# Layer norms in place with GpSimd left only the power, their scale and bias over rows put off to VectorE, and the per-layer input projected from split parts

## The chip, the cores and the metric

The kernel runs on one core of a Trainium2 chip. The metric is the device time of one execution in microseconds (us). The core has TensorE (PE: matmuls, and a separate row for its weight loads, PEld), VectorE (DVE), ScalarE (ACT), GpSimd (POOL), and SyncE (SP), which here only issues transfers.

## The reference

A two-layer decoder on 256 tokens of 1024 channels, in f32. Each layer has a mixer (mLSTM in layer 0, latent attention in layer 1), an expert stage (PEER), and a gated per-layer input. After the mixer and after the expert stage stands a layer norm:

```python
def layer_norm(x, g, b):
    mu = jnp.mean(xf, -1, keepdims=True)
    var = jnp.mean(jnp.square(xf - mu), -1, keepdims=True)
    y = (xf - mu) * lax.rsqrt(var + NORM_EPS)
    return y * g + b
for i in range(DEPTH):
    mix = mlstm_mixer(x, ...) if i < N_A_LAYERS else mla_mixer(x, ...)
    x = layer_norm(DN_ALPHA * x + mix, ln_g[i, 0], ln_b[i, 0])
    x = layer_norm(DN_ALPHA * x + peer_ffn(x, ...), ln_g[i, 1], ln_b[i, 1])
    x = x + jax.nn.sigmoid(x @ ple_w_gate[i]) * (p[i] @ ple_w_proj[i])
```

There are four norms, called N0 (layer 0, after the mixer), N1 (layer 0, after the experts), N2 and N3 (layer 1) below.

## The kernel before

**Numbers.** Every large product is made from two parts of each operand: `split` (L241) casts a weight tile to a rounded part `hi` on ScalarE (L248) and takes the rest, `lo`, by a subtraction (L251), and `mm3` (L258 to L261) adds three matmuls, hi by hi, hi by lo and lo by hi. The subtraction runs on the engine that `lo_engine` names: VectorE, but GpSimd inside a norm.

**Order.** The program is a queue of jobs, `Pipe`. A job is one weight tile's matmuls; its split is issued up to three jobs ahead (`AHEAD`), and a job pushed with `fence=True` (the norms) may not be looked past. After each job its `budget` is spent on fillers: generators that issue one small piece of work at a time. `drain` issues what is left of one. Each engine then works through its instructions in the order in which they were issued.

**Stages.** Per layer: the mixer; the first norm; the query products of the experts (`qps`, over the 8 MB of `w_q`); the top-k and a stage of 64 steps over `u`; a stage of 64 steps over `v` (the value stage, `v_jobs`, four jobs a step, tile `vw`), whose result stays in the four banks `acc`; the second norm, with the projection of the per-layer input `p @ w_pp` inside; and the gate (`gate_jobs`), sixteen jobs over `w_pg` in two halves of eight, each half ended by a sigmoid and two products in `finish` (L1242 to L1244).

**A norm** (`norm_rows`, L419). The two blocks of 128 tokens, tb 0 and tb 1, go through the same steps. `total` (L435) adds ALPHA times the residual to the mixer's or experts' result and writes tile `z`; `stats` takes mean and variance; the power -0.5 is taken on GpSimd (L444); L448 makes -mean times the power. `scale` writes z times the power plus that, for tb 0 on ScalarE (L454) and for tb 1 on VectorE (L452). `turn` transposes eight 128x128 pieces on TensorE (L464), and `first`, `first_rest`, `second` and `second_parts` read them, with the norm's scale and bias now per partition, into the split, transposed `xt` (names x0a, x0b, x1a, x1b with h or l) that the next products read. At the end GpSimd multiplies and adds the scale and bias over the rows of `z` (L538, L539, tile `gb`): these rows are the residual of the next norm, or what the gate is added to. The two or three splits that were issued ahead of the norm have their casts early and their subtractions inside it, on GpSimd.

In a second norm `project` (L1207) makes the four 128x512 products of the per-layer input in plain f32 from `pw` and `pt` (L1210), one ahead of `turn(0)`, one behind it, and two behind `turn(1)`; `keep` copies them out (L1225).

Of the kernel before, what the change touches and what calls it, by code (L numbers as in the profile page):

```python
# [25 lines left out]
D = 1024  # L26
# [137 lines left out]
def tile_trunk(ctx: ExitStack, tc: tile.TileContext, a, out):  # L164
# [74 lines left out]

    lo_engine = Box()  # L240
    lo_engine.v = nc.vector  # L241

    put_off = Box()

    def split(src, n=512, low=None):
        hi = hi4()
        lo = lo4()
        nc.scalar.copy(hi[:, :n], src)  # L248

        def rest():  # L250
            (low or lo_engine.v).tensor_sub(lo[:, :n], src, hi[:, :n].bitcast(F32))  # L251
# [166 lines left out]

    def norm_rows(acc, xres, idx, gb, xt_name, during=()):  # L419

        z = s8("z")
        mvs, sts, banks = {}, {}, {}
# [79 lines left out]
        lows, put_off.v = put_off.v, None  # L502
        lo_engine.v = nc.gpsimd
        total(0, 0)
# [5 lines left out]
        stats(0, 1)  # L510
        lows.pop(0)()
        if not early:
# [8 lines left out]
        stats(1, 1)  # L521
        for fn in lows:
            fn()
        lo_engine.v = nc.vector
        first(0)
# [5 lines left out]
        first_rest(1)  # L531
        second(0)
        second(1)
        second_parts(0)
        second_parts(1)
        during[3]()
        for tb in range(2):
            nc.gpsimd.tensor_mul(rows(tb), rows(tb), gb[:, 0:D])  # L538
            nc.gpsimd.tensor_add(rows(tb), rows(tb), gb[:, D:2 * D])  # L539
        return z, xt  # L540


# [310 lines left out]
    def pre_gb():  # L853
        xres.v = s8("xres")
        load(xres.v, a["x"])
        gbx.v = load_gb(0)

# [3 lines left out]
    def first_norm(idx, name):  # L861
        def run():
            xcur.v, xt.v = norm_rows(acc, xres.v, idx, gbx.v, name)
        return run
# [4 lines left out]

    def peer(l):  # L870
        idx = small([P, 256, 2, 2], "idx", F16)
# [326 lines left out]
    def second_norm(l):  # L1198
        pw, pt = raw("pw"), raw("pt")
        load(pw, a["w_pp"][l])  # L1200
        load(pt[:, 0:512], a["pT"][l])
        if l == 0:
# [4 lines left out]
        def project(tb, hf):  # L1207
            ps = acc_bank()
            for k in range(2):
                nc.tensor.matmul(ps, pt[:, k * 256 + tb * 128:k * 256 + tb * 128 + 128],  # L1210
                                 pw[:, k * D + hf * 512:k * D + hf * 512 + 512], start=(k == 0), stop=(k == 1))
            return ps

        def run():
# [11 lines left out]
            xcur.v, xt.v = norm_rows(acc, xcur.v, 2 * l + 1, gbx.v, "x%db" % l,  # L1226
                                     [step((0, 0)), step((0, 1)), step((1, 0), (1, 1)), keep])
        return run, pp

    def gate_jobs(l, pp, x3):  # L1230

        o = Box()

        def finish(hf, banks):
            if o.v is None:
                o.v = s8("xple")
            if l == 0 and hf == 0:
# [32 lines left out]
        for hf in range(2):  # L1270
            place = pair_of_banks()
            if hf == 0:
                pipe.later(3, lambda: warm(AF.Sigmoid))
            move_jobs(lambda k, n, hf=hf: wgx.v[:, hf * 4096 + k * 512:hf * 4096 + (k + n) * 512],
                      xt, place, list(range(8)), post=lambda hf=hf, place=place: finish(hf, place()),
                      tail=4 if hf else 99)
    def mla(x3):
# [357 lines left out]
```

## Time and profile before

| | |
|---|---|
| median of 3 runs | 1964.25 us (1963.82 to 1964.58) |
| profiled execution | 1963.32 us, its span 1961.2 us |
| TensorE busy | 1903.8 us (97%) |
| VectorE busy | 1486.2 us (76%) |
| ScalarE busy | 1045.2 us (53%) |
| GpSimd busy | 154.1 us (8%) |
| data moved | 336.69 MB, mean 172 GB/s |

All times below are positions and lengths in the span of the profiled execution. The span is cut into stages; in each of them the busy time of an engine divided by the stage's length tells how much room it has. Within a stage the timeline lists the instructions by their start. The bracket at the end of a row is the time for which the engine stood still ahead of it and what let it go on.

### The profile page before, as it was taken

Reading aid. Unit: us, or ns where it says so; the run is one execution under the profiler, and the core shown is the slowest. Engines: PE = TensorE matmul, PEld = TensorE weight load, DVE = VectorE, ACT = ScalarE, POOL = GpSimd, SP = SyncE. Lnnn points to the kernel's source line nnn. Section 1 sums busy time; section 2 is a strip of 40 time slices with the busy share of each in tenths; the row PEclk is TensorE's granted clock in tenths of the full one; section 3 lists DMA queues with packets and bytes.
Section 4 is the critical chain, followed back from the end, with each engine's and each line's share of the span. In section 5 each row is a group of like instructions: output and inputs, shape, how many; then the busy total and the mean of one; then the engine's idle time right before and its main releaser. Section 6 shows DMA issues by size and latency. Waiting matters only on the chain.

```text
span 1961.2 us, 32911 instructions
## 1 busy us (share of the span) xinstructions
PE 1903.8 (97%) x12648; PEld 1713.3 (87%) x12648; DVE 1486.2 (76%) x3100; ACT 1045.2 (53%) x1972; POOL 154.1 (8%) x126
## 2 busy tenths in 40 slices
PE   9989999999999999999899899999999999999997
PEld 7779999999997888888697799899999888888885
DVE  6677999788887666666766789987888866666666
ACT  5555555555445555555564455455554455555554
POOL 0030142000000000000200301510000000000003
PEclk9989999999999999999999899999999999999999
DMA  9241545444434576757143125454444265755550
GB/s 371 102 178 46 185 158 176 169 163 161 163 139 173 193 258 235 259 202 260 62 172 129 43 102 179 151 187 158 162 162 173 101 222 193 279 215 193 193 177 22
DMA packets 50861, 336.69 MB, mean 172 GB/s; under 512 B 5776, under 2 KB 6032, under 8 KB 12688
## 3 DMA queue, kind: packets, MB, share of 16 engines
q1 hardware_dynamic: 50704, 334.59, 47.2%
q8 instruction: 99, 1.62, 0.4%
q14 instruction: 58, 0.48, 0.1%
HBM read 333.52 MB, written 1.05 MB: 171 GB/s over the span
## 4 chain that ended last, share of the span: by engine, by line
issue 67%; PE 18%; DVE 13%; POOL 1%; ACT 0%; DMA 0%; POOLq 0%; SPq 0%; ACTq 0%
DVE lo L251 5%; PE acc L259 2%; PE acc L260 2%; PE acc L261 2%; DVE scr L956 2%; PE qps L297 2%; PE qps L294 2%; PE qps L291 2%; DVE scr L965 1%; DVE z L452 1%; DVE scr L905 1%; PE acc L1010 1%; DVE scr L897 1%; POOL lo L251 1%; DVE scr L902 0%
## 5 line engine op out<-in xcount | busy, mean ns | idle before, releaser
L251 DVE TENSOR_TENSOR lo<-vw,hi 128x512 fp32r<-128x512 f32 x512 | 354.2, 692 | 258.8 <-ACT hi L248 250.6
L248 ACT CAST hi<-vw 128x512 fp32r<-128x512 f32 x512 | 319.3, 624 | 305.4 <-DVE lo L251 267.9
L248 ACT CAST hi<-u 128x512 fp32r<-128x512 f32 x512 | 315.9, 620 | 285.3 <-PE ups L297 255.6
L251 DVE TENSOR_TENSOR lo<-u,hi 128x512 fp32r<-128x512 f32 x512 | 368.8, 729 | 88.9 <-ACT hi L248 86.3
L260 PE MATMUL acc<-lo,wb 128*128 128x512 f32 x1024 | 398.6, 389 | 0.0
L259 PE MATMUL acc<-hi,wb 128*128 128x512 f32 x1024 | 398.4, 389 | 0.0
L261 PE MATMUL acc<-hi,wb 128*128 128x512 f32 x1024 | 398.4, 389 | 0.0
L260 PEld LDWEIGHTS acc<-lo,wb 128*128 128x128 f32 x1024 | 192.2, 188 | 40.4 <-DVE lo L251 0.5
L261 PEld LDWEIGHTS acc<-hi,wb 128*128 128x128 f32 x1024 | 192.2, 188 | 40.0
L259 PEld LDWEIGHTS acc<-hi,wb 128*128 128x128 f32 x1024 | 192.2, 188 | 39.6
L251 DVE TENSOR_TENSOR lo<-h,hi 128x512 fp32r<-128x512 f32 (+2 forms) x178 | 116.2, 665 | 73.6 <-ACT hi L248 71.9
L248 ACT CAST hi<-h 128x512 fp32r<-128x512 f32 (+2 forms) x194 | 115.0, 604 | 105.5 <-PE acc L261 47.7
L294 PE MATMUL ups<-x0ah,lo 128*128 128x256 f32 x1024 | 166.1, 285 | 5.1 <-DVE lo L251 5.1
L294 PE MATMUL ups<-x1ah,lo 128*128 128x256 f32 x1024 | 165.8, 284 | 5.2 <-DVE lo L251 5.2
L291 PE MATMUL ups<-x1ah,hi 128*128 128x256 f32 x1024 | 167.6, 286 | 0.0
L291 PE MATMUL ups<-x0ah,hi 128*128 128x256 f32 x1024 | 167.6, 286 | 0.0
L297 PE MATMUL ups<-x0al,hi 128*128 128x256 f32 x1024 | 164.4, 283 | 0.0
L297 PE MATMUL ups<-x1al,hi 128*128 128x256 f32 x1024 | 164.4, 283 | 0.0
L294 PEld LDWEIGHTS ups<-x0ah,lo 128*128 128x128 f32 x1024 | 141.2, 192 | 7.2 <-DVE lo L251 7.2
L294 PEld LDWEIGHTS ups<-x1ah,lo 128*128 128x128 f32 x1024 | 140.9, 191 | 7.2 <-DVE lo L251 7.2
L291 PEld LDWEIGHTS ups<-x0ah,hi 128*128 128x128 f32 x1024 | 141.3, 192 | 0.0
L291 PEld LDWEIGHTS ups<-x1ah,hi 128*128 128x128 f32 x1024 | 141.2, 192 | 0.0
(357 smaller groups left out, 2662.6 us busy)
## 6 DMA issues: line engine op xcount, KB each, us to landing
u<-u SPq DMA_DIRECT2D x128, 1024.0 KB, 4.8
vw<-v SPq DMA_DIRECT2D x128, 1024.0 KB, 4.8
h<-w_q SPq DMA_DIRECT2D x16, 1024.0 KB, 10.4
h<-w_pg SPq DMA_DIRECT2D x16, 512.0 KB, 5.6
h<-w_v SPq DMA_DIRECT2D x4, 1024.0 KB, 14.3
h<-w_og SPq DMA_DIRECT2D x4, 1024.0 KB, 18.5
h<-w_ao SPq DMA_DIRECT2D x4, 1024.0 KB, 20.6
gb<-lnp SPq DMA_DIRECT2D x4, 1024.0 KB, 5.8
```

What stands on the lines that cost most here:

```text
L248: nc.scalar.copy(hi[:, :n], src)
L251: (low or lo_engine.v).tensor_sub(lo[:, :n], src, hi[:, :n].bitcast(F32))
L259: nc.tensor.matmul(o, lh, rh, start=first, stop=False)
L260: nc.tensor.matmul(o, lh, rl, start=False, stop=False)
L261: nc.tensor.matmul(o, ll, rh, start=False, stop=last)
L291: nc.tensor.matmul(o, hi[:, c:c + 128], x.v.h(k), start=(k == 0), stop=False)
L294: nc.tensor.matmul(o, lo[:, c:c + 128], x.v.h(k), start=False, stop=False)
L297: nc.tensor.matmul(o, hi[:, c:c + 128], x.v.l(k), start=False, stop=(k == nk - 1))
L452: nc.vector.tensor_scalar(v[:, c], v[:, c], mv[:, 2:3], mv[:, 3:4], op0=ALU.mult, op1=ALU.add)
L897: nc.vector.max_index(iu[:, 0:8], v[:, 0:8], s)
L905: nc.vector.max_index(iu[:, 8:16], v[:, 8:16], s)
L956: nc.vector.tensor_tensor(eq, iota[:, None, 0:NCAND].to_broadcast([P, 16, NCAND]), d["pf"][:, h * 16:h * 16 + 16, None].to_broadcast([P, 1 ...
```

## The change

- Norms work in place: `norm_rows` gets the residual tile as `z` and writes its sums back into it, so there is no new tile. L448 goes: tb 0 takes -mean on VectorE (a 128x1 instruction that needs no power) and multiplies it by the power on ScalarE; tb 1 subtracts the mean and multiplies by the power in one instruction.
- GpSimd keeps the power. The subtractions of the splits stay on VectorE: one ahead of `scale(1)`, the others behind `second(0)`.
- The scale and bias over rows become a filler, `affine`, of four VectorE instructions of 128x1024. For N0 and N2 it runs in the value stage of the same layer (`gb` loaded at step 2, used from step 6, and ended by step 32); for N1 and N3 in the gate, whose jobs now have a budget of 900.
- `p @ w_pp` is made with `mm3` from split parts. `w_pp` and `p` are loaded at step 54 of the value stage; `w_pp` is split by a filler from step 58 (four casts, four subtractions), `p` at step 62. The twelve matmuls of tb 0 stand ahead of `turn(0)`, those of tb 1 between `turn(0)` and `turn(1)`, and the copies ahead of `first(1)`.

```diff
-    def norm_rows(acc, xres, idx, gb, xt_name, during=()):
-        z = s8("z")
+    def norm_rows(acc, z, idx, xt_name, during=()):
...
-            nc.vector.scalar_tensor_tensor(rows(tb)[:, c], xres[:, tb * D + hf * 512:tb * D + hf * 512 + 512],
-                                           ALPHA, acc[tb][hf], op0=ALU.mult, op1=ALU.add)
+            nc.vector.scalar_tensor_tensor(rows(tb)[:, c], rows(tb)[:, c], ALPHA, acc[tb][hf],
+                                           op0=ALU.mult, op1=ALU.add)
...
                 nc.gpsimd.tensor_tensor(mv[:, 2:3], mv[:, 1:2], nhalf[:, 0:1], op=ALU.pow)
+                if tb == 0:
+                    nc.vector.tensor_scalar(mv[:, 3:4], mv[:, 0:1], -1.0, None, op0=ALU.mult)
         def scale(tb):
-            nc.vector.scalar_tensor_tensor(mv[:, 3:4], mv[:, 0:1], -1.0, mv[:, 2:3], op0=ALU.mult, op1=ALU.mult)
+            if tb == 0:
+                nc.scalar.activation(mv[:, 3:4], mv[:, 3:4], AF.Copy, scale=mv[:, 2:3])
             for c in (slice(0, 512), slice(512, 1024)):
                 if tb:
-                    nc.vector.tensor_scalar(v[:, c], v[:, c], mv[:, 2:3], mv[:, 3:4], op0=ALU.mult, op1=ALU.add)
+                    nc.vector.tensor_scalar(v[:, c], v[:, c], mv[:, 0:1], mv[:, 2:3],
+                                            op0=ALU.subtract, op1=ALU.mult)
...
-        lo_engine.v = nc.gpsimd
...
-        lows.pop(0)()
...
-        for fn in lows:
-            fn()
-        lo_engine.v = nc.vector
+        lows.pop(0)()
         first(0)
         scale(1)
...
         second(0)
+        for fn in lows:
+            fn()
         second(1)
...
+    def affine(z, gb):
         for tb in range(2):
-            nc.gpsimd.tensor_mul(rows(tb), rows(tb), gb[:, 0:D])
-            nc.gpsimd.tensor_add(rows(tb), rows(tb), gb[:, D:2 * D])
+            v = z[:, tb * D:(tb + 1) * D]
+            nc.vector.tensor_mul(v, v, gb[:, 0:D])
+            yield 1130
+            nc.vector.tensor_add(v, v, gb[:, D:2 * D])
+            yield 1130
...
+        def affine_gen():
+            yield from affine(xcur.v, gbx.v)
+        def load_first():
+            gbx.v = load_gb(2 * l)
+        def use_first():
+            pipe.fillers.append(affs)
         def load_next():
+            pipe.drain(affs)
             gbx.v = load_gb(2 * l + 1)
...
+        def part_gen():
+            ple["wh"], ple["wl"] = s8("pwh", F32R), [xt4("pwl").rearrange("p a b -> p (a b)") for _ in range(2)]
+            for c in range(0, 2048, 512):
+                h, src = ple["wh"][:, c:c + 512], ple["w"][:, c:c + 512]
+                nc.scalar.copy(h, src)
+                nc.vector.tensor_sub(ple["wl"][c // D][:, c % D:c % D + 512], src, h.bitcast(F32))
+                yield 700
...
+            nc.scalar.copy(ple["th"], ple["p"])
+            nc.vector.tensor_sub(ple["tl"], ple["p"], ple["th"].bitcast(F32))
...
+            if pr in (2, 6, 32):
+                pipe.push({2: load_first, 6: use_first, 32: load_next}[pr])
+            if pr in (54, 58):
+                pipe.push(load_ple if pr == 54 else part_ple)
...
+            if pr == 62:
+                pipe.push(part_p)
...
-                nc.tensor.matmul(ps, pt[:, k * 256 + tb * 128:k * 256 + tb * 128 + 128],
-                                 pw[:, k * D + hf * 512:k * D + hf * 512 + 512], start=(k == 0), stop=(k == 1))
+                mm3(ps, ple["th"][:, t], ple["tl"][:, t], ple["wh"][:, c], ple["wl"][k][:, hf * 512:hf * 512 + 512],
+                    k == 0, k == 1)
...
-                                     [step((0, 0)), step((0, 1)), step((1, 0), (1, 1)), keep])
+                             [step((0, 0), (0, 1)), step((1, 0), (1, 1)), keep])
...
+        pipe.push(lambda: pipe.fillers.append(affs))
...
-                      tail=4 if hf else 99)
+                      tail=4 if hf else 99, budget=900.0)
```

VectorE's order in N3, before, from the statistics of tb 1 on (`lnst` and `lnmv` hold the statistics, `xtps` the transposed pieces, `h` is a gate weight tile):

```order
L442 BN_AGGR lnmv<-lnst 128x2
L443 TENSOR_SCALAR lnmv<-lnmv 128x1
L448 SCALAR_TENSOR_TENSOR lnmv<-lnmv 128x1
L452 TENSOR_SCALAR z<-z,lnmv 128x512 x2
L484 TENSOR_TENSOR x1bl_21030<-hi,x1bh_21028 128x4x128
L473 TENSOR_SCALAR hi<-xtps,cols 128x128 x2
L484 TENSOR_TENSOR x1bl_21030<-hi,x1bh_21028 128x4x128
L473 TENSOR_SCALAR lo<-xtps,cols 128x256 x2
L495 TENSOR_TENSOR x1bl_21031<-lo,x1bh_21029 128x512 x2
L251 TENSOR_TENSOR lo<-h,hi 128x512 x10
```

The same place now, where `xple` is the tile of the rows:

```order
L439 BN_AGGR lnmv<-lnst 128x2
L440 TENSOR_SCALAR lnmv<-lnmv 128x1
L248 TENSOR_TENSOR lo<-h,hi 128x512
L452 TENSOR_SCALAR xple<-xple,lnmv 128x512 x2
L485 TENSOR_TENSOR x1bl_21067<-hi,x1bh_21065 128x4x128
L474 TENSOR_SCALAR hi<-xtps,cols 128x128 x2
L485 TENSOR_TENSOR x1bl_21067<-hi,x1bh_21065 128x4x128
L248 TENSOR_TENSOR lo<-h,hi 128x512
L474 TENSOR_SCALAR lo<-xtps,cols 128x256 x2
L496 TENSOR_TENSOR x1bl_21068<-lo,x1bh_21066 128x512 x2
L248 TENSOR_TENSOR lo<-h,hi 128x512 x2
```

L448 is gone, and two of the splits' subtractions stand inside the norm. Behind the last of these rows VectorE's order in the gate was ten subtractions in a row; now it goes on with:

```order
L542 TENSOR_TENSOR xple<-xple,gb 128x1024
L248 TENSOR_TENSOR lo<-h,hi 128x512
L544 TENSOR_TENSOR xple<-xple,gb 128x1024
L248 TENSOR_TENSOR lo<-h,hi 128x512
L542 TENSOR_TENSOR xple<-xple,gb 128x1024
L248 TENSOR_TENSOR lo<-h,hi 128x512
L544 TENSOR_TENSOR xple<-xple,gb 128x1024
L248 TENSOR_TENSOR lo<-h,hi 128x512 x5
```

The four row instructions stand between the subtractions for the first half's jobs 4 to 7.

TensorE's order in N3, before, from the value stage's end to the gate's first product:

```order
L1210 MATMUL acc<-pw,pt 128x512 x2
L464 MATMUL xtps<-ident,z 128x128 x8
L1210 MATMUL acc<-pw,pt 128x512 x2
L464 MATMUL xtps<-ident,z 128x128 x8
L1210 MATMUL acc<-pw,pt 128x512 x4
L259 MATMUL acc<-hi,x1bh_21028 128x512
```

The same place now: the last two of tb 1's four triples (hi by hi, hi by lo, lo by hi of one half of the contraction), the second `turn`, and the gate's first product:

```order
L256 MATMUL acc<-pwh,pt 128x512
L257 MATMUL acc<-pwl,pt 128x512
L258 MATMUL acc<-pwh,pt 128x512
L256 MATMUL acc<-pwh,pt 128x512
L257 MATMUL acc<-pwl,pt 128x512
L258 MATMUL acc<-pwh,pt 128x512
L465 MATMUL xtps<-ident,xple 128x128 x8
L256 MATMUL acc<-hi,x1bh_21065 128x512
```

Nothing of the projection stands behind the second `turn` any more.

## Rows read from the trace of the kernel before

**Rows 1.** The page, busy time of each engine.
```profile
PE 1903.8 (97%) x12648; PEld 1713.3 (87%) x12648; DVE 1486.2 (76%) x3100; ACT 1045.2 (53%) x1972; POOL 154.1 (8%) x126
```
**Rows 2.** Stages: length, busy PE, PEld, DVE, ACT, POOL; clock, DMA, GB/s.
```profile
112.00:136.00 24.00, 15.67 (x69) 12.32 (x67) 20.42 (x25) 11.04 (x21) 15.96 (x10) 0.72 0.29 117
1600.00:1900.00 300.00, 300.00 (x1325) 248.43 (x1324) 186.21 (x277) 166.10 (x276) 0.00 (x0) 1.00 0.59 212
```
**Rows 3.** Timeline of N3: start, length, engine, line, operation, tiles, [idle, releaser].
```profile
1916.27 0.39 PE L261 MATMUL acc<-hi,wb 128*128 128x512 f32 x1
1920.51 0.55 POOL L444 TENSOR_TENSOR lnmv<-lnmv,nhalf 128x1 f32<-128x1 f32 x1 [2.44 <-DVE lnmv L443]
1921.02 1.27 POOL L251 TENSOR_TENSOR lo<-h,hi 128x512 fp32r<-128x512 f32 x1
1921.09 1.22 DVE L448 SCALAR_TENSOR_TENSOR lnmv<-lnmv 128x1 f32<-128x1 f32 x1 [0.66 <-POOL lnmv L444]
1922.25 2.35 POOL L538 TENSOR_TENSOR z<-z,gb 128x1024 f32<-128x1024 f32 x1
1922.34 5.02 DVE L452 TENSOR_SCALAR z<-z,lnmv 128x512 f32<-128x512 f32 x2
1924.67 2.41 POOL L539 TENSOR_TENSOR z<-z,gb 128x1024 f32<-128x1024 f32 x1
1927.42 1.11 PE L464 MATMUL xtps<-ident,z 128*128 128x128 f32 x4 [1.32 <-DVE z L452]
1928.33 5.24 PE L1210 MATMUL acc<-pw,pt 128*128 128x512 f32 x8
1929.35 2.18 DVE L484 TENSOR_TENSOR x1bl<-hi,x1bh 128x512 fp32r<-128x512 f32 x1 [0.74 <-ACT x1bh L480]
1932.36 2.54 DVE L495 TENSOR_TENSOR x1bl<-lo,x1bh 128x512 fp32r<-128x512 f32 x2
1933.63 0.50 PE L259 MATMUL acc<-hi,x1bh 128*128 128x512 f32 x1
1935.59 2.50 DVE L251 TENSOR_TENSOR lo<-h,hi 128x512 fp32r<-128x512 f32 x4 [0.69 <-ACT hi L248]
```
**Rows 4.** Timeline, ScalarE: the first half's sigmoid behind N3.
```profile
1945.36 1.08 ACT L1242 ACTIVATE xple<-acc 128x512 f32<-128x512 f32 x2
```
**Rows 5.** Stretches of 1 us in N3 and behind N0, columns as in rows 2.
```profile
1924.00:1925.00 1.00, 0.00 (x0) 0.01 (x1) 1.00 (x2) 0.00 (x0) 0.92 (x2) 0.90 0.00 0
1931.00:1932.00 1.00, 1.00 (x3) 0.42 (x2) 1.00 (x3) 0.00 (x0) 0.94 (x1) 0.68 0.00 0
136.00:137.00 1.00, 1.00 (x8) 0.89 (x7) 1.00 (x3) 0.42 (x2) 0.00 (x0) 0.89 0.00 0
```
**Rows 6.** Timeline of N0.
```profile
123.82 5.02 DVE L452 TENSOR_SCALAR z<-z,lnmv 128x512 f32<-128x512 f32 x2
130.84 1.22 PE L291 MATMUL qps<-x0ah,hi 128*128 128x256 f32 x4 [0.83 <-ACT x0ah L480]
133.83 2.57 DVE L495 TENSOR_TENSOR x0al<-lo,x0ah 128x512 fp32r<-128x512 f32 x2
```
**Rows 7.** Timeline of N2 and of N1.
```profile
1097.52 1.22 PE L291 MATMUL qps<-x1ah,hi 128*128 128x256 f32 x4 [0.83 <-ACT x1ah L480]
...
961.96 5.44 PE L1210 MATMUL acc<-pw,pt 128*128 128x512 f32 x8
967.26 0.50 PE L259 MATMUL acc<-hi,x0bh 128*128 128x512 f32 x1
```
**Rows 8.** VectorE's groups by line and shape: count, busy us, mean ns.
```profile
L956 DVE TENSOR_TENSOR scr<-iota,scr 128x800 f32<-128x800 f32 x32 | 34.5, 1078 | 0.0
L452 DVE TENSOR_SCALAR z<-z,lnmv 128x512 f32<-128x512 f32 x8 | 20.1, 2549 | 0.1
L448 DVE SCALAR_TENSOR_TENSOR lnmv<-lnmv 128x1 f32<-128x1 f32 x8 | 9.7, 1213 | 3.5 <-POOL lnmv L444 3.3
L705 DVE TENSOR_SCALAR hn<-hn,mc,mn 128x128 f32<-128x128 f32 x8 | 2.4, 342 | 0.1
```

More of the change, by code (lines that the diff above doesn't have):

```diff
@@ L238, in warm @@
             nc.scalar.activation(t, nhalf[0:1, 0:1], fn)
-    lo_engine = Box()
-    lo_engine.v = nc.vector
     put_off = Box()
@@ L250, in rest @@
         def rest():
-            (low or lo_engine.v).tensor_sub(lo[:, :n], src, hi[:, :n].bitcast(F32))
+            (low or nc.vector).tensor_sub(lo[:, :n], src, hi[:, :n].bitcast(F32))
         if put_off.v is None:
@@ L536, in norm_rows @@
         during[3]()
+        return xt
+    def affine(z, gb):
         for tb in range(2):
-            nc.gpsimd.tensor_mul(rows(tb), rows(tb), gb[:, 0:D])
-            nc.gpsimd.tensor_add(rows(tb), rows(tb), gb[:, D:2 * D])
-        return z, xt
+            v = z[:, tb * D:(tb + 1) * D]
[3 more added lines that the diff above has]
+            yield 1130
     qk = Box()
@@ L855, in pre_gb @@
         load(xres.v, a["x"])
-        gbx.v = load_gb(0)
     pipe.push(pre_gb)
@@ L862, in run @@
         def run():
-            xcur.v, xt.v = norm_rows(acc, xres.v, idx, gbx.v, name)
+            xt.v = norm_rows(acc, xres.v, idx, name)
+            xcur.v = xres.v
         return run
@@ L868, in reset_acc, with peer @@
             r[0] = r[1] = None
-    def peer(l):
+    def peer(l, ple):
         idx = small([P, 256, 2, 2], "idx", F16)
@@ L1166, in v_jobs, with load_ple, part_p, part_ple @@
                     pipe.push(main, prep, None, budget)
+        def affine_gen():
[4 more added lines that the diff above has]
+            pipe.fillers.append(affs)
         def load_next():
+            pipe.drain(affs)
             gbx.v = load_gb(2 * l + 1)
+        affs = affine_gen()
+        def load_ple():
+            if l == 0:
+                ple["p"], ple["w"] = wbx.v[:, 7168:7680], wax.v[:, 6144:8192]
+            else:
+                t = big("ple")
+                ple["p"], ple["w"] = t[:, 0:512], t[:, 1024:3072]
+            load(ple["w"], a["w_pp"][l])
+            load(ple["p"], a["pT"][l])
+        def part_gen():
[5 more added lines that the diff above has]
+                yield 700
+        def part_p():
+            pipe.drain(parts)
+            t = raw("pt", F32R)
+            ple["th"], ple["tl"] = t[:, 0:512], t[:, 512:1024]
+            nc.scalar.copy(ple["th"], ple["p"])
+            nc.vector.tensor_sub(ple["tl"], ple["p"], ple["th"].bitcast(F32))
+        parts = part_gen()
+        def part_ple():
+            pipe.fillers.append(parts)
         def start_v():
@@ L1194, in peer, with second_norm @@
                 pipe.push(lambda: pipe.drain(ropes))
+            if pr == 62:
+                pipe.push(part_p)
     wgx, wax, wbx, wrx = Box(), Box(), Box(), Box()
[L1198 to L1201, printed above, removed]
+    def second_norm(l, ple):
         if l == 0:
@@ L1209, in project @@
             for k in range(2):
-                nc.tensor.matmul(ps, pt[:, k * 256 + tb * 128:k * 256 + tb * 128 + 128],
-                                 pw[:, k * D + hf * 512:k * D + hf * 512 + 512], start=(k == 0), stop=(k == 1))
+                t = slice(k * 256 + tb * 128, k * 256 + tb * 128 + 128)
+                c = slice(k * D + hf * 512, k * D + hf * 512 + 512)
+                mm3(ps, ple["th"][:, t], ple["tl"][:, t], ple["wh"][:, c], ple["wl"][k][:, hf * 512:hf * 512 + 512],
+                    k == 0, k == 1)
             return ps
@@ L1225, in keep @@
                     nc.scalar.copy(pp.v[:, tb * D + hf * 512:tb * D + hf * 512 + 512], ps)
-            xcur.v, xt.v = norm_rows(acc, xcur.v, 2 * l + 1, gbx.v, "x%db" % l,
-                                     [step((0, 0)), step((0, 1)), step((1, 0), (1, 1)), keep])
+            xt.v = norm_rows(acc, xcur.v, 2 * l + 1, "x%db" % l,
+                             [step((0, 0), (0, 1)), step((1, 0), (1, 1)), keep])
         return run, pp
@@ L1232, in gate_jobs, with affine_gen @@
         o = Box()
+        def affine_gen():
+            yield from affine(xcur.v, gbx.v)
+        affs = affine_gen()
+        pipe.push(lambda: pipe.fillers.append(affs))
         def finish(hf, banks):
             if o.v is None:
+                pipe.drain(affs)
                 o.v = s8("xple")
@@ L1524, in pre @@
             xres.v = xcur.v
-            gbx.v = load_gb(2)
         pipe.push(pre)
@@ L1529, in tile_trunk @@
     for l in range(DEPTH):
-        peer(l)
-        run, pp = second_norm(l)
+        ple = {}
+        peer(l, ple)
+        run, pp = second_norm(l, ple)
         pipe.push(run, fence=True)
```

3 lines of the change are left out of this document (removed).

## The prediction

> **What bounds the kernel now.** I read the page first, then stage windows, then the timeline of one norm, then groups by shape. TensorE is busy 97% of the span [rows 1], but that average hides the norms: in the 24 us around N0 it is busy 15.67, at a mean granted clock of 0.72, while in 300 us of the value stage it never stops, and 300 us hold 1325 products, 0.227 us each [rows 2]. The room is in the four norms.
>
> In N3 the timeline shows what stands there. The second power ends at 1921.06 (1920.51 + 0.55). Then VectorE takes 1.22 us for L448, a 128x1 instruction, and 5.02 for two L452 of 128x512. Beside them GpSimd works: L448 starts at 1921.09 and ends at 1922.31, GpSimd's subtraction runs from 1921.02 to 1922.29; the two L452 end at 1927.36, GpSimd's L538 and L539 end at 1924.60 and 1927.08. L484 takes 2.18, where subtractions of its size take 0.63 each once GpSimd is done (2.50 for four at 1935.59) [rows 3]. L448 costs 1213 ns, while L705, a VectorE instruction of the same form as L452 (two scalars per partition) on a quarter of the elements, costs 342, and L452 2549 [rows 8]. So these lengths are GpSimd's, not the work's own: VectorE waits for GpSimd's instruction. TensorE gets its last transposes only at 1927.42 and then does 5.24 us of the f32 projection before the gate's first product at 1933.63 [rows 3]. Its clock falls to 1.2 GHz while it stands still (the granted share is 0.90 in the microsecond from 1924, half of it behind that) and is back in that from 1931 [rows 5].
>
> On this the Trainium skill has a rule ("SBUF — State Buffer", section "Who interferes with whom"): VectorE with two SBUF inputs, or in a two-port mode, and GpSimd reading SBUF exclude each other for a whole instruction. These trace rows agree: the ends of L448 and L452 stand 0.02 to 0.28 us behind those of GpSimd's work. It also speaks against one place of the change, the subtraction that now stands right behind the variance of tb 1, beside GpSimd's power: one of the two would wait in full, by it 0.6 us a norm where I take 0.3 below, a total of 1946.6.
>
> **Durations for after.** A `scale(1)` instruction without GpSimd beside it is not in the trace. The low bound is L705's 342 ns on a quarter of the elements, the high one the 2.55 us of today. I take 0.5, near L705's, since GpSimd's ends explain the rest. A row instruction of 128x1024 has its bounds at 1.08 (L956, 128x800, VectorE) [rows 8] and 2.41 (the same work on GpSimd) [rows 3]; I take 1.2, L956 with some more elements. A subtraction of 128x512 is 0.63 in a row and up to 0.69 alone. Eight transposes I take as 0.95 at full clock (four took 1.11 at half).
>
> **N3.** The split of `p` (a cast and a subtraction at the end of the value stage) puts off its last `vw` split: the last product, at 1916.27 before [rows 3], ends about 1917.1, 0.6 later. TensorE then has twelve products (12 x 0.227 = 2.7) to 1919.8, transposes to 1920.8, twelve more to 1923.5, transposes to 1924.45. VectorE has L448 no more (1.2 us twice, one of them ahead of tb 1's statistics), puts one subtraction beside the power, waits about 0.3 for it, and ends `scale(1)` at about 1922.3, before TensorE asks. So the gate's first product comes at 1924.45 instead of 1933.63, 9.2 earlier.
>
> Not all of that stays. The first half of the gate is eight jobs of six products, 10.9 us: TensorE alone would end it at 1935.4. But VectorE now carries the subtractions GpSimd did and the four row instructions. Its L485 for tb 1 starts about 1.9 behind the start of the second four transposes, as before (1927.42 to 1929.35) [rows 3], so at 1925.9. Then come seven pieces of 0.63 to 0.69 (two shifts counted as one and a half) up to the split of job 3, 4.7 us, and four times a row instruction and a subtraction, 4 x (1.2 + 0.63) = 7.3: job 7's `lo` is there at 1937.9, and its last five products end at 1939.0. Before, they ended at 1944.5 (the sigmoid starts at 1945.36 [rows 4]; 1933.63 + 10.9). **Gain 5.5**; VectorE keeps 3.7 of the 9.2. The second half runs as before.
>
> **N1.** Its rows stand like N3's (961.96 for the projection, 967.26 for the gate's first product [rows 7], against 1928.33 and 1933.63). Behind the first half layer 0 has more VectorE work (the split of the layer's result). I take **4.5**.
>
> **N0 and N2.** No projection stands here, and the next products need both token blocks. In N0 two L452 from 123.82 [rows 6] become two of 0.5 (-4.0), L448 of tb 1 goes (-1.2), L448 of tb 0 goes ahead of the last sum, less the wait for the power (-0.5): the first query product moves from 130.84 to 125.1. `x0al`, ready at 136.40 before (133.83 + 2.57) [rows 6], comes at about 128.6, early enough. The clock rises in the microsecond from 136 [rows 5], 5.4 us behind the first product; I let it rise as much behind the new one. Taking 0.7 off for the second subtraction that VectorE now has there: **5.0**. N2's first product, at 1097.52 [rows 7], waits for the same cast as N0's: **5.0**.
>
> **What is added elsewhere.** In the value stage each layer gets four row instructions, 4.8 us, and five subtractions, 3.2. VectorE is busy 186.21 of 300 us there [rows 2], and splits are issued three jobs (4.1 us) ahead, longer than any one filler: I take nothing. Without that cover it would be 2 x 8.0 = 16 us. ScalarE's five casts a layer lie in 166.10 of 300. The loads of `gb` and `w_pp` are moved, not added, in a stage with a DMA share of 0.59 [rows 2]; on SP's queue they stand between `v` loads that are issued ahead, and I take nothing. The extra eight products a layer's projection (24 of 0.227 us instead of 16 f32 passes) are in the 2.7 us pieces.
>
> **Sum.** 5.5 + 4.5 + 5.0 + 5.0 = 20.0; less 0.3 a norm for the power beside the subtraction where it was not yet counted in full, 1.2: 18.8. The profiled execution took 1963.32 (span 1961.2, the rest around it unchanged), 0.93 under the median of the runs shown. 1963.32 - 18.8 = 1944.5; at the level of the median, **1945.4 us**.
>
> **Rivals.**
>
> *The clock stays low as long as today.* TensorE still stands still in N0 and N2 (about 122.5 to 125), so the clock may fall at the same place and rise at 136 whatever TensorE does before. Then 11 us instead of 5.4 run at half clock, and N0 and N2 lose 2.8 each; in N1 and N3 the gate starts later, about one each. Sum 18.8 - 7.6 = 11.2, time **1953**. For it: each fall today lasts until TensorE has worked for a while. Against: in N3 and N1 the twelve-product pieces fill most of the pause.
>
> *The clock does not fall at all*, since the pause is shorter. N0 and N2 gain 1.9 more each: **1941.6**.
>
> *L452 is slow by itself.* Then `scale(1)` stays near 2.5 twice, N0 and N2 keep 1.0 each, the gate starts some 4 later and VectorE's chain with it, N3 keeps 3.2 and N1 2.3. Sum 7.5 less 0.8: **1957.5**. Against it stands L705 [rows 8].
>
> *Something else is late in N0 and N2*, the `w_q` weights, which come on the same queue: the query products start earlier and wait. N0 and N2 give nothing: **1955.4**. Stage windows show a DMA share of 0.29 in N0 [rows 2], which speaks against.
>
> *VectorE's row instructions are dear and become the gate's bound* (the slower side). Between the gate's splits each microsecond above 1.2 goes straight to TensorE: eight of them at a price p cost 8 x (p - 1.2). The gain is gone at p = 3.5; at 4.0, 22.4 is lost against 18.8: **1968**. For it: GpSimd needs 2.41 for one, and the instruction reads and writes the same tile. Against: L956's 1.08 with two inputs of nearly that size.
>
> **How the numbers follow.** The forecast 0.67, on its own from 1942 to 1950; the clock as long as today 0.12, never falling 0.08, L452 slow by itself 0.04, late weights 0.04, row instructions dear 0.05 (about 0.03 of it above the break-even). The range from 1939.5 to 1955 leaves out the dear sides and holds the clock either way. About 0.2% (4 us) is what a measurement tells from no change. Faster by more: 0.92; within: 0.04; slower: 0.04.
>
> **What the changed profile would show.** `scale(1)`'s two instructions at about 0.5 us each, the row instructions at 1.2; the gate's first product some 7.4 us behind the value stage's last (17.0 before); the first query product 5.7 us earlier against the mixer's end; in the first half of the gate TensorE waiting for VectorE's `lo`; no new pause of TensorE between steps 6 and 62 of the value stage. The prediction is wrong if `scale(1)` stays above 2 us, if row instructions take over 2, if TensorE stands still in the value stage, or if the low clock in N0 lasts as it does now.

## The result, and the profile after

The changed kernel takes 1939.13 us (median of 4 runs, 1937.26 to 1939.90), the kernel before beside it 1964.41; the ratio is 0.987 (0.985 to 0.989). It is 25.3 us faster where 18.8 were forecast, and lies 0.4 below the forecast range. The profiled pair differs by less, 23.4 (1963.32 to 1939.90; the profiled run of the changed kernel was the longest of its four, that of the kernel before shorter than the four beside it); a repetition (below) gave 26.2.

The page of the changed kernel, busy time of each engine; [rows 1] is its counterpart:

```profile
PE 1896.5 (98%) x12664; PEld 1713.5 (88%) x12664; DVE 1477.7 (76%) x3130; ACT 1051.2 (54%) x1986; POOL 106.3 (5%) x102
```

GpSimd lost 48 us of work, and VectorE, which took it over, is busy 8.5 us *less* than before. Its busy time before held waiting. Stages (length, busy PE, PEld, DVE, ACT, POOL; clock, DMA share, GB/s), against [rows 2]:

```profile
112.00:130.00 18.00, 14.97 (x69) 12.23 (x68) 14.18 (x28) 11.41 (x23) 4.09 (x4) 0.82 0.21 84
1588.00:1888.00 300.00, 300.00 (x1325) 248.51 (x1324) 191.56 (x284) 168.48 (x280) 0.00 (x0) 1.00 0.59 213
```

Around N0 TensorE still does 69 instructions, now in 18 us. In the value stage it does its 1325 products in 300 us as before, with 5 us more of VectorE beside them. The timeline of N3, against [rows 3] and [rows 4]; the positions are of the changed kernel's own span, in which the value stage ends at 1900.09:

```profile
1902.69 0.68 DVE L248 TENSOR_TENSOR lo<-h,hi 128x512 fp32r<-128x512 f32 x1
...
1902.85 0.93 POOL L441 TENSOR_TENSOR lnmv<-lnmv,nhalf 128x1 f32<-128x1 f32 x1 [2.52 <-DVE lnmv L440]
...
1903.81 1.00 DVE L452 TENSOR_SCALAR xple<-xple,lnmv 128x512 f32<-128x512 f32 x2 [0.44 <-POOL lnmv L441]
...
1906.41 1.03 PE L465 MATMUL xtps<-ident,xple 128*128 128x128 f32 x8
...
1907.20 0.48 PE L256 MATMUL acc<-hi,x1bh 128*128 128x512 f32 x1
...
1908.64 0.69 DVE L485 TENSOR_TENSOR x1bl<-hi,x1bh 128x512 fp32r<-128x512 f32 x1 [1.09 <-ACT x1bh L481]
...
1908.66 0.50 PE L256 MATMUL acc<-hi,x1bh 128*128 128x512 f32 x1 [0.52 <-ACT x1bh L481]
...
1912.08 0.50 PE L256 MATMUL acc<-hi,x1bh 128*128 128x512 f32 x1 [0.66 <-ACT hi L245]
...
1913.35 1.22 DVE L542 TENSOR_TENSOR xple<-xple,gb 128x1024 f32<-128x1024 f32 x1
...
1922.44 1.08 ACT L1298 ACTIVATE xple<-acc 128x512 f32<-128x512 f32 x2
```

The two L452 are 1.00 together instead of 5.02, L485 0.69 instead of 2.18, a row instruction 1.22 (GpSimd: 2.35 to 2.41). The gate's first product stands 7.11 behind the value stage's end, where it stood 16.97 behind. N0, against [rows 6], and the clock behind it, against [rows 5]:

```profile
121.64 0.96 POOL L441 TENSOR_TENSOR lnmv<-lnmv,nhalf 128x1 f32<-128x1 f32 x1 [2.21 <-DVE lnmv L440]
122.64 1.00 DVE L452 TENSOR_SCALAR xres<-xres,lnmv 128x512 f32<-128x512 f32 x2 [0.45 <-POOL lnmv L441]
...
123.33 1.90 PE L465 MATMUL xtps<-ident,xres 128*128 128x128 f32 x8 [1.30 <-DVE xres L452]
...
125.92 1.22 PE L288 MATMUL qps<-x0ah,hi 128*128 128x256 f32 x4 [0.69 <-ACT x0ah L481]
```

```profile
123.00:124.00 1.00, 0.67 (x4) 0.70 (x5) 1.00 (x3) 0.35 (x1) 0.00 (x0) 0.70 0.00 0
129.00:130.00 1.00, 1.00 (x7) 1.00 (x6) 1.00 (x2) 1.00 (x3) 0.00 (x0) 0.50 0.00 0
130.00:131.00 1.00, 1.00 (x9) 1.00 (x9) 0.51 (x2) 0.34 (x2) 0.00 (x0) 0.89 0.00 0
```

The clock falls to 1.2 GHz in the microsecond from 123 and is back in that from 130, not 136: it is low for 6.8 us where it was low for 13.7, in N2 as in N0. In N1 and N3 it no longer falls (1.00 granted from 945 to 957 and from 1895 to 1907).

For the runs below, the span is cut at TensorE's own instructions: N0 and N2 from the end of the mixer's last product to the first `u` product, N1 and N3 from the end of the value stage's last product to the end of the gate's last, and one value stage (us, from the timelines of one profiled execution each; the `u` stages and the mixers differ by up to 1.5). e7_gpsimd_beside was executed once, so it has no interval.

| run | N0 | N1 | N2 | N3 | sum | value stage | median | ratio to before, 95% interval |
|---|---|---|---|---|---|---|---|---|
| before | 67.5 | 40.0 | 68.2 | 39.5 | 215.2 | 348.3 | | |
| after | 61.1 | 33.6 | 62.0 | 33.0 | 189.7 | 348.9 | 1939.13 | 0.9869 (0.9852 to 0.9886) |
| e1_again | 60.4 | 33.6 | 62.0 | 33.0 | 188.9 | 348.9 | 1938.48 | 0.9870 (0.9853 to 0.9886) |
| e2_rows_on_gpsimd | 68.7 | 39.1 | 69.5 | 39.1 | 216.3 | 349.0 | 1964.27 | 0.9999 (0.9989 to 1.0008) |
| e3_f32_projection | 60.4 | 33.7 | 60.6 | 33.0 | 187.7 | 348.3 | 1936.91 | 0.9863 (0.9846 to 0.9879) |
| e4_no_rows | 60.4 | 32.9 | 60.8 | 32.2 | 186.2 | 348.9 | 1935.61 | 0.9854 (0.9838 to 0.9871) |
| e5_before_rows_moved | 63.1 | 35.1 | 63.0 | 34.4 | 195.5 | 348.4 | 1944.51 | 0.9898 (0.9882 to 0.9915) |
| e6_lo_on_gpsimd | 61.9 | 33.1 | 62.8 | 32.3 | 190.1 | 348.9 | 1938.98 | 0.9869 (0.9853 to 0.9886) |
| e7_gpsimd_beside | 59.8 | 35.0 | 61.4 | 34.3 | 190.5 | 348.9 | 1938.98 | |
| e8_fill_pause | 59.8 | 33.6 | 60.2 | 32.9 | 186.5 | 348.9 | 1935.91 | 0.9855 (0.9838 to 0.9871) |
| e9_lo_later | 61.0 | 34.3 | 61.4 | 33.6 | 190.2 | 348.9 | 1939.59 | 0.9872 (0.9856 to 0.9888) |
| e10_rows_in_norm | 66.1 | 39.6 | 66.8 | 39.1 | 211.5 | 348.9 | 1961.43 | 0.9985 (0.9975 to 0.9994) |
| e11_best | 60.2 | 34.1 | 60.5 | 33.4 | 188.2 | 348.3 | 1937.33 | 0.9860 (0.9844 to 0.9876) |
| e12_fill_f32 | 59.8 | 33.7 | 60.2 | 32.9 | 186.6 | 348.3 | 1935.42 | 0.9852 (0.9835 to 0.9868) |

### The profile page after: what moved, and what is told of

The parts are those of the page before. It is cut to its first block, busy times and chain, and to the rows that moved or that the text cites. A ratio compares the mean times of both kernels' runs of the same rounds, so it can differ in the third digit from the quotient of the medians.

```text
span 1938.1 us, 32931 instructions
## 1 busy us (share of the span) xinstructions
PE 1896.5 (98%) x12664; PEld 1713.5 (88%) x12664; DVE 1477.7 (76%) x3130; ACT 1051.2 (54%) x1986; POOL 106.3 (5%) x102
## 4 chain that ended last, share of the span: by engine, by line
PE 82%; DVE 15%; issue 2%; ACT 2%; DMA 0%; POOL 0%; SPq 0%; ACTq 0%; POOLq 0%; DVEq 0%
PE acc L257 14%; PE acc L256 14%; PE acc L258 14%; PE ups L288 9%; PE ups L291 9%; PE ups L294 9%; DVE lo L248 6%; PE gps L1077 3%; PE qps L288 2%; PE qps L291 2%; DVE scr L960 2%; PE qps L294 2%; DVE scr L969 1%; DVE scr L909 1%; PE acc L1014 1%
## 5 line engine op out<-in xcount | busy, mean ns | idle before, releaser
L258 PEld LDWEIGHTS acc<-hi,wb 128*128 128x128 f32 x1024 | 192.3, 188 | 39.5
L248 DVE TENSOR_TENSOR lo<-h,hi 128x512 fp32r<-128x512 f32 (+2 forms) x186 | 121.8, 666 | 67.6 <-ACT hi L245 65.4
L294 PEld LDWEIGHTS ups<-x1al,hi 128*128 128x128 f32 x1024 | 141.6, 192 | 0.0
```

Source lines behind the costliest of these rows:

```text
L248: (low or nc.vector).tensor_sub(lo[:, :n], src, hi[:, :n].bitcast(F32))
L258: nc.tensor.matmul(o, ll, rh, start=False, stop=last)
L294: nc.tensor.matmul(o, hi[:, c:c + 128], x.v.l(k), start=False, stop=(k == nk - 1))
```

## The experiments

**e1_again**, unchanged.

> The changed kernel once more, to size it beside the others. The two profiles differ by 23.4 us (1963.32 to 1939.90), the two medians by 25.3. If the medians are right, 25 us under the kernel before; if the profiled pair is, 23 to 24.

Measured: 1938.48 (1937.87 to 1939.78), 26.2 under the kernel before. The stage sums say the same: the norms give 25.5 to 26.2, two value stages take back 1.2.

**e2_rows_on_gpsimd**: the row instructions alone go back.

```diff
         during[3]()
+        for tb in range(2):
+            nc.gpsimd.tensor_mul(rows(tb), rows(tb), gbx.v[:, 0:D])
+            nc.gpsimd.tensor_add(rows(tb), rows(tb), gbx.v[:, D:2 * D])
         return xt
```

> The changed kernel with the scale and bias over rows back on GpSimd at the end of each norm; all else stays changed. Theory 1 (VectorE waits for GpSimd's whole instructions, and that is most of the gain): the two scale(1) instructions go from 1.0 us together back to about 5, the first query product in N0 comes some 5 us later behind the mixer's end, N0 and N2 lose 5 each, N1 and N3 2 to 4 each, 14 to 18 in all. Theory 2 (the gain of N1 and N3 is the projection's, that of N0 and N2 is L448's): scale(1) stays under 1.5, the loss is under 4.

Measured: 1964.27, the whole gain is gone (25.8 lost, 14 to 18 expected). Theory 2 falls: scale(1) is 5.05 again. N0's timeline also shows what the expectation lacked, the subtraction that the change had put on VectorE now waiting for GpSimd too:

```profile
122.21 2.34 POOL L537 TENSOR_TENSOR xres<-xres,gb 128x1024 f32<-128x1024 f32 x1
122.27 5.05 DVE L452 TENSOR_SCALAR xres<-xres,lnmv 128x512 f32<-128x512 f32 x2 [0.45 <-POOL lnmv L441]
...
131.03 2.69 POOL L538 TENSOR_TENSOR xres<-xres,gb 128x1024 f32<-128x1024 f32 x1
131.41 2.85 DVE L248 TENSOR_TENSOR lo<-h,hi 128x512 fp32r<-128x512 f32 x1
```

A subtraction of 0.69 takes 2.85. All the other edits together are worth nothing that the runs can tell (0.9989 to 1.0008) while GpSimd has the rows.

**e3_f32_projection**: the projection's products, loads, order and copies as before.

```diff
-                mm3(ps, ple["th"][:, t], ple["tl"][:, t], ple["wh"][:, c], ple["wl"][k][:, hf * 512:hf * 512 + 512],
-                    k == 0, k == 1)
+                nc.tensor.matmul(ps, pt[:, k * 256 + tb * 128:k * 256 + tb * 128 + 128],
+                                 pw[:, k * D + hf * 512:k * D + hf * 512 + 512], start=(k == 0), stop=(k == 1))
```

> The changed kernel with the per-layer input again projected in plain f32, with its loads, its order and its copies as before. Theory 1: N0 and N2 unchanged, the gate's first product some 3 to 5 us later in N1 and N3, the value stage 0.6 shorter; if TensorE sets the gate's first half the loss is 2 to 4 a norm, 4 to 8 in all. If VectorE's four row instructions set the gate's first half, as the forecast had it, most of that is hidden: 0 to 2 in all.

Measured: 1936.91, not slower; it is 1.6 under e1_again, but the runs overlap (1936.16 to 1938.61, 1937.87 to 1939.78). In the traces the two value stages are 1.2 shorter, 0.6 each; N2 is 1.3 shorter too, but there the clock was low for 3.4 us instead of 6.8. The gate's first product is 10.1 behind the value stage's end instead of 7.0, in N1 and in N3, and the gate then runs 3.0 faster: the last gate product comes at the same distance (33.7 and 33.0). In N3:

```profile
1901.66 3.60 PE L1256 MATMUL acc<-pw,pt 128*128 128x512 f32 x8
...
1906.44 0.50 PE L256 MATMUL acc<-hi,x1bh 128*128 128x512 f32 x1 [1.18 <-ACT pp L1271]
```

The gate's first six jobs run here almost without a wait, and the last two of its first half wait for VectorE's `lo` as they do in the changed kernel (shown below e4_no_rows). So an earlier TensorE does not end the gate's first half earlier; the split projection gains nothing there, and its own splitting costs the value stage 0.6 each time.

**e4_no_rows**: the fillers are not pushed, so the scale and bias over rows are left out.

```diff
-        pipe.push(lambda: pipe.fillers.append(affs))
+
-            if pr in (2, 6, 32):
-                pipe.push({2: load_first, 6: use_first, 32: load_next}[pr])
+            if pr in (2, 32):
+                pipe.push({2: load_first, 32: load_next}[pr])
```

> The changed kernel with the scale and bias over rows left out everywhere (the residual rows lack them). The forecast has VectorE's four row instructions take 3.7 us of each gate's first half: without them 7 us faster. The changed kernel's trace shows no wait of TensorE behind job 2 of the gate: by that, under 1 us. The value stage gives 0 by both.

Measured: 1935.61, 2.9 under e1_again. The gates give 0.7 to 0.8 each, not 3.7, the value stages nothing; another 1.2 stands in N2's query products, where the clock was low for 3.4 us instead of 6.8. TensorE's matmuls wait in N3, by line (us in total, times, longest), in the same three places with the rows and without; this is the changed kernel:

```profile
PE acc L256 <- ACT hi L245: 0.7, 1, 0.7
PE acc L256 <- ACT x1bh L481: 0.5, 1, 0.5
PE acc L257 <- DVE lo L248: 0.3, 1, 0.3
```

What holds the gate's first jobs is the hand-over of the norm's own result and the casts of the gate's weights behind it on ScalarE. From the first gate product (1907.20) to that of job 2 (1912.08) two jobs, 2.7 us of products, take 4.9; the first three jobs lose 2.9, with the rows and without.

What the rows cost stands in the weight loads, not in the list above. In the changed kernel those of jobs 6 and 7 wait for `lo`:

```profile
1918.70 0.19 PEld L257 LDWEIGHTS acc<-lo,x1bh 128*128 128x128 f32 x1 [0.50 <-DVE lo L248]
...
1920.43 0.19 PEld L257 LDWEIGHTS acc<-lo,x1bh 128*128 128x128 f32 x1 [0.51 <-DVE lo L248]
```

These two jobs are 0.4 longer each than the ones ahead of them. Without the rows neither waits, and that is the 0.8 of N3. The expectation's "no wait of TensorE behind job 2" had passed them over.

**e5_before_rows_moved**: the kernel before with the rows moved and nothing else.

```diff
         second_parts(1)
         during[3]()
-        for tb in range(2):
-            nc.gpsimd.tensor_mul(rows(tb), rows(tb), gb[:, 0:D])
-            nc.gpsimd.tensor_add(rows(tb), rows(tb), gb[:, D:2 * D])
-        return z, xt
+        return z, xt
```

> The kernel before with one part of the change alone: the scale and bias over rows as a VectorE filler in the value stage and the gate; L448, the subtractions on GpSimd, the separate tile and the f32 projection stay. Theory 1 (GpSimd's row instructions hold VectorE): the two L452 fall from 5.02 us to about 1.0, L448 stays at 1.2 beside GpSimd's subtraction; N0 and N2 gain 4 to 5 each up to the first query product, N1 and N3 3 to 5 each; 15 to 20 in all, 1945 to 1950. Theory 2 (each part holds back the others, so that the change works only as a whole): under 8.

Measured: 1944.51, 20 of the 25 to 26. L452 is 1.00, L448 still ends with GpSimd's subtraction:

```profile
122.60 1.26 POOL L251 TENSOR_TENSOR lo<-h,hi 128x512 fp32r<-128x512 f32 x1
122.67 1.22 DVE L448 SCALAR_TENSOR_TENSOR lnmv<-lnmv 128x1 f32<-128x1 f32 x1 [0.68 <-POOL lnmv L444]
...
123.92 1.00 DVE L452 TENSOR_SCALAR z<-z,lnmv 128x512 f32<-128x512 f32 x2
```

The first query product of N0 is 8.01 behind the mixer's end, between 11.70 before and 5.96 in e1_again: moving the rows gives 3.7, the rest of the change 2.

**e6_lo_on_gpsimd**: the subtractions inside the norm go back to GpSimd.

```diff
+        lo_engine.v = nc.gpsimd
         total(0, 0)
...
+        lows.pop(0)()
         if not early:
...
-        lows.pop(0)()
+        for fn in lows:
+            fn()
+        lo_engine.v = nc.vector
         first(0)
```

> The changed kernel with the subtractions of the splits inside the norms back on GpSimd, where they stood before. Theory 1: GpSimd's subtraction (1.27 us) starts when the power ends, so scale(1) starts 1.3 later behind the power, less the 0.7 that VectorE saves and the 0.4 by which the power was stretched: N0 and N2 0.2 to 1 us later at the first query product; 1 to 4 in all. Rival: VectorE is short of time behind the norm, and handing the subtractions to GpSimd makes it 1 to 3 faster.

Measured: 1938.98, the same within the noise. Each theory holds in its place, neither in all: N0 and N2 are 1.5 and 0.8 longer than in e1_again, N1 and N3 0.5 and 0.6 shorter. Of the 1.5 and 0.8, 0.5 and 0.9 stand ahead of the first query product, as theory 1 had it; in both norms the clock was also low for 3.4 us longer than in e1_again.

**e7_gpsimd_beside**: two GpSimd instructions that nothing waits for.

```diff
+                if tb == 1 and idx % 2:
+                    s = spare.v.rearrange("p t a b -> p (t a b)")
+                    nc.gpsimd.tensor_tensor(s, s, s, op=ALU.subtract)
+                    nc.gpsimd.tensor_tensor(s, s, s, op=ALU.subtract)
```

> The changed kernel with two instructions more on GpSimd behind the power of tb 1 in N1 and N3, on a tile that nothing else uses any more (128x1024, each minus itself, f16). No instruction waits for them by a semaphore. If VectorE is held by GpSimd's use of memory ports, the two scale(1) instructions go from 1.0 us to 3 or more in N1 and N3 and stay 1.0 in N0 and N2. If the 5.02 of the kernel before came from the tile that both engines worked on, they stay 1.0 everywhere.

Measured, in N3:

```profile
1901.53 1.89 POOL L445 TENSOR_TENSOR gts<-gts 128x1024 f16<-128x1024 f16 x1
1901.59 4.14 DVE L457 TENSOR_SCALAR xple<-xple,lnmv 128x512 f32<-128x512 f32 x2 [0.44 <-POOL lnmv L442]
...
1903.49 1.96 POOL L446 TENSOR_TENSOR gts<-gts 128x1024 f16<-128x1024 f16 x1
```

The two instructions of scale(1) end 0.28 behind GpSimd's second, 4.14 us for 1.00 of work, with no tile in common. That VectorE waits for GpSimd's whole instruction is shown. Of the 3.1 us less than half reaches TensorE: the gate's first product is 1.2 to 1.3 later in N1 and N3, and the gate's end 1.3 to 1.4. The single time (1938.98) shows little of these 2.7: N0 and N2 are 0.6 shorter each than in e1_again, and the rest is within what executions of one kernel differ by. In N0, where the code is the changed kernel's own, the clock did not fall at all in this execution.

**e8_fill_pause**: idle matmuls in TensorE's pauses of N0 and N2.

```diff
+            def keep_on(n):
+                def f():
+                    ps = acc_bank("idle")
+                    for i in range(n):
+                        nc.tensor.matmul(ps[:, 0:128], ident, ident, start=True, stop=True)
+                return f
-            xt.v = norm_rows(acc, xres.v, idx, name)
+            xt.v = norm_rows(acc, xres.v, idx, name, [keep_on(4), keep_on(6), keep_on(6)])
```

> The changed kernel with idle matmuls (128x128, identity by identity, into a bank that nothing reads) in the three pauses of TensorE in N0 and N2: four ahead of the first turn, six behind each turn. If the clock falls there because TensorE stands still, the granted clock stays at 1.0 in both norms, the query products next to them run at full clock, and N0 and N2 give 1.5 to 3 us each: 3 to 6 in all. If the fall has another reason it stays, and the idle matmuls cost 0 to 1.

Measured: 1935.91, 2.6 under e1_again. The clock stays up, here in two of the microseconds in which it was low:

```profile
123.00:124.00 1.00, 1.00 (x11) 1.00 (x10) 1.00 (x4) 0.54 (x2) 0.00 (x0) 1.00 0.00 0
128.00:129.00 1.00, 0.73 (x7) 0.53 (x5) 1.00 (x2) 1.00 (x3) 0.00 (x0) 1.00 0.00 0
```

N0 gives 0.6, less than expected, and N2 1.8. N0 had less to give: its clock was low for 3.4 us in e1_again, 6.8 in the profile after. And at full clock TensorE waits for VectorE and ScalarE instead (0.73 busy in the second row, with both of them busy throughout).

The runs with the same code in N0 and N2 sort by how long the clock was low there. N0 takes 59.8 where it never was (e7_gpsimd_beside without idle matmuls, e8_fill_pause and e12_fill_f32 with them), 60.4 with 3.4 us of it (e1_again, e3_f32_projection, e4_no_rows) and 61.1 with 6.8 (after). N2 takes 60.2 (e8_fill_pause, e12_fill_f32), 60.6 to 60.8 (e3_f32_projection, e4_no_rows) and 61.4 to 62.0 (e7_gpsimd_beside, e1_again, after) with the same lengths. So a microsecond at half clock costs 0.1 to 0.3, and e7_gpsimd_beside shows two things more: the idle matmuls themselves cost N0 nothing, and the fall does not come in every execution without them.

**e9_lo_later**: the subtraction beside the power moves behind second(0).

```diff
         stats(1, 1)
-        lows.pop(0)()
         first(0)
```

> The changed kernel with the one subtraction that stands beside the power of tb 1 moved behind second(0) with the other. The power is 0.93 us there instead of 0.55: without the subtraction it should be 0.55 again, scale(1) about 0.4 to 0.7 earlier, and the first query product of N0 and N2 as much; N1 and N3 unchanged, since TensorE asks later. 0.8 to 1.5 faster in all. Rival: what is taken from scale(1) comes back as a late lo of the first query job, and nothing changes.

Measured: 1939.59, no gain. The power is 0.56 again, and the first query product of N0 is 0.16 earlier, of N2 0.33. The rival is right, and more: the first gate job now waits 2.32 us for its `lo`, and each gate is 0.6 to 0.7 later.

```profile
1909.52 0.50 PE L257 MATMUL acc<-lo,x1bh 128*128 128x512 f32 x1 [2.32 <-DVE lo L248]
```

**e10_rows_in_norm**: e2_rows_on_gpsimd with `nc.vector` in place of `nc.gpsimd`.

```diff
+            nc.vector.tensor_mul(rows(tb), rows(tb), gbx.v[:, 0:D])
+            nc.vector.tensor_add(rows(tb), rows(tb), gbx.v[:, D:2 * D])
```

> The changed kernel with the four row instructions on VectorE, but not put off: they stand at the end of each norm, where GpSimd had them. It tells the engine from the time. Theory 1: scale(1) stays at 1.0 us and the first query product where it is; behind that the next splits wait 4.9 us for VectorE, of which three jobs ahead hide a part: N0, N2 and the two gates lose 1 to 4 each, 4 to 14 in all, and most of the gain of 25 stays. Rival: that the rows are put off is what counts, the engine does not matter: loss above 18, as with GpSimd.

Measured: 1961.43; 23 of the gain are lost, as the rival had it. In N0 scale(1) stays short and the first query product where it was (5.95), but the four rows then stand ahead of the splits:

```profile
121.86 1.00 DVE L452 TENSOR_SCALAR xres<-xres,lnmv 128x512 f32<-128x512 f32 x2 [0.45 <-POOL lnmv L441]
...
128.34 1.22 DVE L537 TENSOR_TENSOR xres<-xres,gb 128x1024 f32<-128x1024 f32 x1
...
133.86 0.74 PE L291 MATMUL qps<-x0ah,lo 128*128 128x256 f32 x4 [4.00 <-DVE lo L248]
```

TensorE waits 4.00 us there and 5.1 in each gate. That the rows are put off counts for more than which engine does them: at the norm's end VectorE is 2.8 better than GpSimd (e2_rows_on_gpsimd), and putting them off on VectorE is worth 23. No run put them off and left them on GpSimd.

**e11_best** and **e12_fill_f32** put edits together: e11_best those of e3_f32_projection, e8_fill_pause and e9_lo_later, e12_fill_f32 the first two alone.

```diff
-            xt.v = norm_rows(acc, xres.v, idx, name)
+            xt.v = norm_rows(acc, xres.v, idx, name, [keep_on(4), keep_on(6), keep_on(6)])
...
-                             [step((0, 0), (0, 1)), step((1, 0), (1, 1)), keep])
+                                     [step((0, 0)), step((0, 1)), step((1, 0), (1, 1)), keep])
```

> The changed kernel with three edits together: idle matmuls in the pauses of N0 and N2, the projection again in plain f32 as before, the subtraction away from the power. From the runs so far: 2.6 for the first, 1.6 for the second, 0.8 for the third, 5 in all under the changed kernel's 1938.5: 1933 to 1934. If the three share the same time (the pause is shorter, and so is the stretch at half clock), 1935 to 1936.

> The changed kernel with idle matmuls in the pauses of N0 and N2 and the projection again in plain f32; the subtraction beside the power stays where the change has it. If the run before this one was held back by its later subtraction (a late lo costs 0.7 in each gate and in the query products), the two gains add: 2.6 + 1.6 under 1938.5, 1934 to 1935. If the idle matmuls and the f32 projection take from each other, it is no faster than the better of the two alone, 1936.

Measured: 1937.33, a miss by either case, and 1935.42, between its two cases. The later subtraction costs in the gates here too (34.1 and 33.4 against 33.7 and 32.9). e12_fill_f32 has the lowest median of full kernels, 28.9 under the kernel before and 3.1 under e1_again. Against e8_fill_pause it is 0.5, which the runs don't tell apart (1933.81 to 1935.93 and 1935.37 to 1936.36); the trace has its two value stages 1.2 shorter.

## Why the prediction was too small

**Right.** scale(1) was forecast at 0.5 an instruction and took 0.50; a row instruction at 1.2 and took 1.22; the gate's first product 7.4 behind the value stage's end, 7.1 measured; N0's first query product 5.7 earlier against the mixer's end, 5.5 measured; the value stage without a new wait, and 0.6 longer for the split operands of the projection (e3_f32_projection takes the 0.6 back). That GpSimd holds VectorE is shown by e7_gpsimd_beside. The likeliest case came true, with its sum too small. Neither rival on the clock came true: it was low for half as long as before, and where it never fell (e8_fill_pause) the stage sum is 3.2 under the profile after. A product is 0.226 (300 us by 1325), not 0.227, which moves no sum.

**The step that failed.** The forecast took 3.6 us off its sum for what VectorE takes over: 0.7 in N0 and in N2 for the second subtraction, 1.0 in N1, and 0.3 a norm for the subtraction beside the power. The runs show none of these in the time. The four norms gave 24.3 where 18.8 stood, and the 3.6 is the greater part of the 5.5 between. Against the stage table (after, less 0.6 in N1 and N3 for the value stage):

- N0 and N2, 5.0 each: 6.4 and 6.1 measured. The first query product comes 5.5 and 6.0 earlier, and the query stage behind it did not get longer by 0.7 but shorter (55.8 to 54.8 and 55.7). With that subtraction on GpSimd N2's query stage is no shorter (55.6 in e6_lo_on_gpsimd and in e1_again, the low clock ending 5.9 and 6.0 behind the first product). I had let the clock come back 5.4 us behind the first product in N0; by the same reading it came back 4.3 behind it, and in N2 6.2, where it had been 4.7.
- N1, 4.5: 5.8 measured. I had taken one microsecond off for layer 0's VectorE work behind the first half. N1 gains what N3 gains: from the value stage's end to the first half's sigmoid 28.7 before and 22.3 after, in both.
- N3, 5.5: 5.9 measured.
- The power beside the subtraction, 1.2 off the sum: the power does stretch, from 0.55 to 0.93 or 0.96, but that is inside the distances above, and e9_lo_later shows that taking it away gains nothing. For N1 and N3 my own working had scale(1) done before TensorE asks, so there was no reason for their share. The 0.6 a norm worked out from the Trainium skill's rule ("SBUF — State Buffer", "Who interferes with whom") is not borne out in size (0.4); that one waits for the other is.

In the profiled pair 1.2 of the 24.3 is lost elsewhere (0.5 ahead of N0, 0.7 in layer 1's `u` stage). The medians of the runs are nearer to the 24.3.

**Right in the number, with a limit left out.** The forecast had TensorE ready 9.2 earlier in N3 and VectorE's chain, with its four row instructions, keep 3.7 of that. 9.3 and 3.5 were measured (16.97 to 7.11, less the 0.6 of the value stage; 5.8 at the first half's sigmoid). The sign it named is there too, TensorE waiting for `lo` in jobs 6 and 7. But e4_no_rows gets back only 0.7 to 0.8 a gate without the rows, not 3.7: a second limit, which the forecast left out, lies that close behind the first. It is the norm's own hand-over on ScalarE and VectorE, the 2.9 us that the first three jobs lose. e3_f32_projection starts the gate 3 later, loses almost nothing in those jobs and ends at the same place. So 3 us of the 9.3, which the split projection seems to win, were never on the path.

**What the forecast did not see.** It summed the parts as if each had its price. They don't add: the rows alone give 20 (e5_before_rows_moved), all else alone nothing (e2_rows_on_gpsimd), together 25 to 26. And it put the gain down to GpSimd leaving; e10_rows_in_norm shows that the same rows on VectorE in the same place lose almost as much. What the gain rests on is where the rows now stand. The forecast named the cover of the value stages (16 us without it), but not as a part of the gain. e10_rows_in_norm loses 4.8 to 5.7 in N0 and in N2, whose rows the changed kernel puts under the value stage, and 6.0 to 6.1 in each gate, where it has them one at a time between the subtractions.

**Open.** The 6 us between e5_before_rows_moved and the changed kernel are not shown for any one edit. The projection (e3_f32_projection) and the subtractions (e6_lo_on_gpsimd) give nothing of it when put back alone, which leaves L448 and the norm in place, and no run puts those back. Why the clock was low for 0, 3.4 or 6.8 us in executions of the same code is open too. The profiled pair differs by 1.9 less than the medians; the four runs of the changed kernel alone lie 2.6 apart.

## What to carry to other kernels

Work that only a later stage reads should not stand at a hand-over between stages, on whatever engine: first look for a stage with spare time on one engine and put it there, then ask which engine. When an instruction of one engine ends again and again within a few tenths of another engine's, read its length as a wait, and look for its length elsewhere. Before making a product faster, put it back or leave it out once: the time to the next stage's end, not to its first instruction, tells whether it was on the path.

## What the runs showed of the hardware

- A VectorE tensor_scalar of 128x512 takes 0.50 us; beside an unrelated GpSimd instruction it ends only when that one has (4.14 for two, e7_gpsimd_beside). It goes the other way too: GpSimd's 128x1 power takes 0.93 to 0.96 instead of 0.55 beside a 0.69 us subtraction on VectorE.
- TensorE's clock stayed at 2.4 GHz through N0 and N2 in all three runs with idle matmuls in its pauses (e8_fill_pause, e11_best, e12_fill_f32). Without them it fell to 1.2 GHz in every other profile of the table, in both norms, but for N0 in e7_gpsimd_beside. Filling the pauses was worth 2.4 us by the stage sums: 0.1 to 0.3 for a microsecond at half clock, as TensorE then waits for VectorE and ScalarE instead (0.73 busy in the row of e8_fill_pause).
- The last four f32 matmuls of the projection, which the profile records as eight, took 3.60 us at full clock (e3_f32_projection), 5.24 in the kernel before [rows 3], in part at half.
